# A four-layer trunk on one core: group 0 of each squared-ReLU layer as plain products, and the attention's output projection in three parts

## The chip, the cores and the metric

The kernel runs on one core of one Trainium2 chip. The metric is the device time of one execution in microseconds (us), lower is better. TensorE (PE) does the matmuls and writes them to the accumulators (PSUM); VectorE (DVE) and ScalarE (ACT) read those and do everything elementwise; SyncE (SP) issues most DMAs. Each engine works through its own queue in order.

## The reference, cut to what matters

Input x has 512 frames of 1024 features. Four residual layers follow each other: attention, squared-ReLU MLP, a recurrent block, squared-ReLU MLP, and at the end a norm. Each sub-layer sees rmsnorm(h), and its output is added to h.

```
def sq_relu_mlp(h, w1, w2):
    z = jax.nn.relu(jnp.einsum('bsd,df->bsf', h, w1))    # 1024 -> 4096
    return jnp.einsum('bsf,fd->bsd', z * z, w2)          # 4096 -> 1024

# attention: 16 heads of 64; o holds all heads, w_o is 1024 x 1024
    return jnp.einsum('bsd,de->bse', o, w_o)

for layer in range(2):
    hn = rmsnorm(h, norm_mix[layer])
    h = h + mix(hn)            # attention in layer 0, the recurrent block in layer 1
    h = h + sq_relu_mlp(rmsnorm(h, norm_mlp[layer]), mlp_w1[layer], mlp_w2[layer])
```

All is float32.

## The kernel before, in words

The residual h lies transposed in eight tiles hT[k] of 128 features x 512 frames (KT = 8, T = 512, U = 256, P = 128). To keep float32 accuracy in the faster matmul type, every operand is split into a high half H (rounded, made by ScalarE) and a low half L (the rest, made by VectorE), and every product is three matmuls: H by H, H by L, L by H. This is mm3, lines 176 to 178, which is why nearly all matmuls carry these lines. The names say which product it is: p for the MLP's up products, d for its down products, wo and ro for the two output projections, qk and v for the attention's projections, s, x and oa for the attention's scores, transposes and sums.

**Weights.** A list, plan, holds all weight units of the program in the order of use. fetch takes the next one: a DMA on SP's queue, the high half wh by ScalarE (line 118), the low half wl by VectorE (line 119). A plain unit is 1024 numbers a partition: four k of 256 columns. The units wait in five slots of the pool wsp; in an MLP there are slots of a second pool, wx, too, and of every nine units the last four go there. want(n) takes n units for a matmul group and first prefetches until state["ahead"] more are ready. state["stop"] is the place in the plan at which the prefetch halts until the next stage sets it anew.

**The MLP.** mlp runs over eight groups g of 512 hidden features. up(g) makes the group's hidden features z; down(g-1, m) for eight m adds the group before to hT[m]. They alternate, so that TensorE has down products while VectorE and ScalarE finish z. up uses a Strassen-like scheme (Winograd's form): features and frames are cut in two, and seven products of 256 columns (names "1" to "7") take the place of eight. For this some units of weights are sums of blocks, which VectorE adds beforehand (kinds s1 to s4, lines 115 and 116, tiles b, in the single-buffered pool sr), and the moving operands of some products are sums of blocks of the normed input (sums_of, tiles tH and tL). One of the four sums, t1, is made in the norm's split instead: with blocks=True, lines 204 to 207 write the difference of the two halves of frames into the second half of hnH and hnL for the first four k. The products are put together by seven adds on VectorE, rectified and scaled by rstd r (relu2, line 577), squared, and split.

**The norm.** Norm.feed(k) splits hT[k] times the gain as soon as it is complete. The squares (square, line 220) are added into one tile (nm1acc in layer 0, nm2acc in layer 1); sums adds them over the features with eight tiny matmuls (nm1ss), and rstd turns the result into a row (nm1row). The up products do without rstd until they are rectified. In layer 0's and layer 1's MLP sums and rstd are called inside up(0), and mlp begins with prefetch(4), the four sums_of and then the eight squares.

**The attention.** For head i the loop calls score(i), turn(i-1) (softmax's transposes) and weigh(i-2) (the products with v). After each of the three it calls fill(FILL), which hands a credit to a queue of other matmul work: the projections for later heads and the output projection. A step of a qk or wo projection (three matmuls of 512 columns) costs 2 credits, one of v (three of 256) costs 1. An item of the queue starts only when a head has been reached (its gate); need(name) forces an item to its end.

```
queue += wo_("woA", (0, 1, 2, 3), U, False) + wo_("woB", (4, 5, 6, 7), U, True)
```

woA multiplies the first four head pairs by their rows of w_o and adds the result to hT; its gate is weigh(7). woB does the last four pairs, its gate is weigh(15), the last head; after each of its outputs it feeds the MLP's norm.

The order of the instructions on each engine is laid out at compile time by a program, which starts from the order of these calls and moves an instruction when what it needs isn't there yet. The order quoted in times below is the one that ran.

Of the kernel before, what the change touches and what calls it, by code (L numbers as in the profile page):

```python
# [10 lines left out]
F32 = mybir.dt.float32  # L11
# [4 lines left out]
P = 128  # L16
# [8 lines left out]

FILL = 7.6

# [13 lines left out]
def trunk(ctx: ExitStack, tc: tile.TileContext, xT, cols, win, wqkv, wo, rwin, rga, rgx, rwo, w1, w2, out):  # L41
# [44 lines left out]
    def fetch():  # L86
# [4 lines left out]
        if state["more"] is not None:  # L91
            pool = state["more"] if state["units"] % 9 >= 5 else wsp
            state["units"] += 1
# [58 lines left out]
    def add_mlp(layer):  # L152
        starts.append(len(plan))
        for g in range(9):
            if g < 8:
                rows, cs = (slice(0, T), slice(T, D)), (slice(g * T, g * T + U), slice(g * T + U, (g + 1) * T))
                srcs = [w1[layer][rows[k], cs[c]] for k, c in ((0, 0), (0, 1), (1, 1), (1, 0))]
                up_ = [(kind, 4, srcs) for kind in ("11", "s1", "12", "22", "s2", "s4", "s3")]
            else:
                up_ = []  # L160
            dn = [("plain", 4, [w2[layer][(g - 1) * T : g * T, u * U : (u + 1) * U]]) for u in range(4)] if g else []
            if up_ and dn:
                plan.extend(up_[0:2] + dn[0:1] + up_[2:3] + dn[1:2] + up_[3:5] + dn[2:3] + up_[5:7] + dn[3:4])
            else:
                plan.extend(up_ + dn)

# [5 lines left out]
    add_mlp(1)  # L172
    state["stop"] = starts[0]

# [16 lines left out]
    class Norm:  # L191
        def __init__(self, name, gain, c0=0, n=T, blocks=False):
            self.name, self.gain, self.acc, self.last, self.c, self.n = name, gain, None, None, slice(c0, c0 + n), n
            self.blocks, self.psum = blocks, mmp if blocks else atp

        def split(self, k):
            g = cst[:, self.gain + k : self.gain + k + 1]
            if not self.blocks or k >= KT // 2:
                S.activation(hnH[k], hT[k], AF.Copy, scale=g)
                V.scalar_tensor_tensor(hnL[k], hT[k], g, f(hnH[k]), ALU.mult, ALU.subtract)  # L200
                return

            d = wk.tile([P, T], F32, name=f"{self.name}d{k}", tag="nsq", bufs=2)[:, :U]
            V.tensor_sub(d, hT[k][:, LO], hT[k][:, HI])
            for src, c in ((hT[k][:, LO], LO), (d, HI)):
                S.activation(hnH[k][:, c], src, AF.Copy, scale=g)
                V.scalar_tensor_tensor(hnL[k][:, c], src, g, f(hnH[k][:, c]), ALU.mult, ALU.subtract)

# [13 lines left out]
        def feed(self, k):  # L222
            if k == 0:
                tc.keep_in_program_order(S.activation(spare, epsb, AF.Sqrt))
            self.split(k)
            if not self.blocks:
                self.square(k)


        def sums(self):  # L230
            nt = self.n // P
            ss = self.psum(f"{self.name}ss")
            parts = [self.acc] if self.last is None else [self.acc, self.last]
            for t in range(nt):
                for n, part in enumerate(parts):
                    PE.matmul(
                        ss[:, 2 * t : 2 * t + 2], part[:, t * P : (t + 1) * P], ones[:, 0:2],
                        start=n == 0, stop=n == len(parts) - 1,
                    )
            S.activation(rt[:, :nt], ss[:, 0 : 2 * nt : 2], AF.Sqrt, bias=epsb, scale=1.0 / D)  # L240
            V.reciprocal(rt[:, :nt], rt[:, :nt])

        def rstd(self):
            nt = self.n // P
            row = self.psum(f"{self.name}row")
# [10 lines left out]
    nm1 = Norm("nm1", C_MLP0, blocks=True)  # L256
    with ExitStack() as actx:
# [214 lines left out]
        for i in range(NH + 2):  # L472
# [17 lines left out]
            fill(FILL)  # L490
        need("woB")

# [37 lines left out]
    def mlp(ly, norm, nxt, halves):  # L530
        with ExitStack() as mctx:
            pool = lambda name, bufs: mctx.enter_context(tc.tile_pool(name=f"{name}{ly}", bufs=bufs))
            sr, wx, tp, cp, zp = pool("sr", 1), pool("wx", 4), pool("t", 1), pool("c", 1), pool("z", 2)
            state.update(raw=sr, more=wx, units=0, ahead=7, stop=starts[ly + 1] if ly + 1 < len(starts) else None)
            prefetch(4)
            z, r, tH, tL = {}, [], [], []

            def sums_of(k):
                g, g2 = (cst[:, norm.gain + j : norm.gain + j + 1] for j in (k, k + 4))
                a = wk.tile([P, T], F32, name=f"ha{ly}{k}", tag="nsq", bufs=2)  # L540
                S.activation(a, hT[k], AF.Copy, scale=g)
                H = tp.tile([P, 3, U], F32R, name=f"tH{ly}{k}", tag=f"tH{k}")
                L = tp.tile([P, 3, U], F32R, name=f"tL{ly}{k}", tag=f"tL{k}")
                raw = cp.tile([P, 2, T], F32, name=f"ht{ly}{k}", tag="cB" if k % 2 else "cA")
                raw = raw.rearrange("p i (j c) -> p (i j) c", j=2)

                V.scalar_tensor_tensor(raw[:, 2], hT[k + 4][:, HI], g2, a[:, HI], ALU.mult, ALU.subtract)
                V.tensor_add(raw[:, 1], raw[:, 2], a[:, LO])
                V.scalar_tensor_tensor(raw[:, 0], hT[k + 4][:, LO], g2, raw[:, 1], ALU.mult, ALU.subtract)
                S.activation(H[:, 0:2], raw[:, 0:2], AF.Copy, scale=-1.0)  # L550
                V.scalar_tensor_tensor(L[:, 0:2], raw[:, 0:2], -1.0, f(H[:, 0:2]), ALU.mult, ALU.subtract)  # L551
                S.copy(H[:, 2], raw[:, 2])
                V.tensor_sub(L[:, 2], raw[:, 2], f(H[:, 2]))
# [10 lines left out]
            B11, t1, B21, B22 = own(0, LO), own(0, HI), own(4, LO), own(4, HI)  # L564
            t4, t2, t3 = (sum_(n) for n in range(3))

# [8 lines left out]

            def relu2(g, n, c, op, rr_):
                V.scalar_tensor_tensor(c, c, 0.0, rr_[:, None, :].to_broadcast([P, 2, T]), op, ALU.mult)
                S.activation(c, c, AF.Square)
# [4 lines left out]
                for i in range(2):  # L583
                    z[g, 2 * n + i] = (zH[:, i], zL[:, i])

            def up(g):

                acc = {}

                def one(n, xs):  # L590
                    acc[n] = (mmp if g == 0 and n in "54" else atp)(f"p{n}{ly}{g}")
                    product(acc[n], xs)
                    acc[n] = pair(acc[n])
# [19 lines left out]
                V.tensor_add(cA[:, :, HI], acc["3"], cA[:, :, HI])  # L613
                relu2(g, 0, cA, ALU.max, r[0])
                yield
# [3 lines left out]
                V.tensor_add(cB[:, :, HI], acc["5"], w)  # L619
                relu2(g, 1, cB, ALU.min, r[0])  # L620
                yield
# [59 lines left out]

    nm2 = Norm("nm2", C_MLP1, blocks=True)
    with ExitStack() as rctx:
# [172 lines left out]
```

## Time and profile before

| what | value |
|---|---|
| median of 3 runs | 1104.23 us (1103.11 to 1105.21) |
| the profiled execution's own time | 1108.84 us |
| its span | 1107.1 us |
| mean granted TensorE clock | 0.989 |
| weight units fetched as plain in the MLPs | 64 (512 KB each) |
| weight blocks fetched to be summed in the MLPs | 64 (512 KB each) |

The profile comes from one execution, so sums are made against 1108.84 us. In a view of stretches each row has the window, its length, then for each engine the busy time and the number of instructions, the TensorE clock that was granted (PEclk, 1.00 is full speed), the share of the DMA engines and GB/s. With a tile's name as filter only instructions that touch this tile are counted. Matmuls are pipelined: one lasts longer than the step to the next, so the step from start to start is what counts, and a "busy" TensorE can be slow. The group lines have line, engine, operation, output<-input, shapes, count, then busy us and mean ns of one, then the idle time before them with what ended it. The waits have total us, number of times and the longest.

### The profile page before, as it was taken

How to read it: one execution, taken by the hardware profiler on the slowest of the kernel's cores; microseconds unless marked ns; L12 is line 12 of the kernel's file. 1: busy time of each engine (PE TensorE's matmuls, PEld its weight loads, DVE VectorE, ACT ScalarE, POOL GpSimd, SP SyncE). 2: the span in 40 equal slices, each digit the busy share in tenths (PEclk: the TensorE clock that was granted, in tenths of full speed). 3: DMA queues.
4: the chain of work that ended last, by engine and by line, in shares of the span. 5: the costliest groups of instructions: out<-in, count | busy, mean ns of one | idle time of the engine just before them, and what ended most of it. 6: DMA issues, size and time to landing. Idle time of an engine off the chain costs nothing.

```text
span 1107.1 us, 16096 instructions
## 1 busy us (share of the span) xinstructions
PE 1080.5 (98%) x6424; PEld 962.2 (87%) x6424; DVE 875.9 (79%) x1316; ACT 538.5 (49%) x794; POOL 11.0 (1%) x28
## 2 busy tenths in 40 slices
PE   9999999997999999999999999899999999999996
PEld 7889988887899899999988888789899999899996
DVE  7998888788886886777767689988897786777655
ACT  7766665465443443433435497456453343343321
POOL 1000000000000000000000000000000000000000
PEclk9999999998999999999999999999999999999998
DMA  8532441332334324313241122432433333323102
GB/s 266 136 101 72 115 118 55 109 100 77 100 92 152 96 62 138 105 58 115 59 151 58 58 76 77 123 124 82 129 107 103 116 95 94 106 82 99 57 1 77
DMA packets 113786, 109.10 MB, mean 99 GB/s; under 512 B 4016, under 2 KB 110640, under 8 KB 113712
## 3 DMA queue, kind: packets, MB, share of 16 engines
q1 hardware_dynamic: 113568, 108.02, 32.2%
q8 instruction: 50, 0.82, 0.3%
q14 instruction: 24, 0.20, 0.1%
q10 hardware_dynamic: 144, 0.07, 0.0%
HBM read 101.78 MB, written 2.10 MB: 94 GB/s over the span
## 4 chain that ended last, share of the span: by engine, by line
PE 82%; DVE 11%; DMA 3%; ACT 2%; issue 2%; SPq 0%; DVEq 0%; ACTq 0%
PE d L176 10%; PE d L177 10%; PE d L178 10%; PE p L176 9%; PE p L178 9%; PE p L177 9%; DVE wl L119 2%; PE x L384 1%; PE xb L176 1%; PE xb L178 1%; PE xb L177 1%; ACT wh L118 1%; DMA wr<-in_wqkv 1%; PE v L176 1%; PE oa L400 1%
## 5 line engine op out<-in xcount | busy, mean ns | idle before, releaser
L118 ACT CAST wh<-b 128x1024 fp32r<-128x1024 f32 x112 | 115.9, 1049 | 203.1 <-DVE b L116 76.8
L177 PE MATMUL d<-zL,wh 128*128 128x512 f32 (+1 forms) x544 | 205.9, 379 | 0.0
L176 PE MATMUL d<-zH,wh 128*128 128x512 f32 (+1 forms) x544 | 205.3, 380 | 0.0
L178 PE MATMUL d<-zH,wl 128*128 128x512 f32 (+1 forms) x544 | 204.7, 377 | 0.0
L119 DVE TENSOR_TENSOR wl<-b,wh 128x1024 fp32r<-128x1024 f32 x112 | 135.6, 1223 | 48.0 <-ACT wh L118 48.0
L118 ACT CAST wh<-wr 128x1024 fp32r<-128x1024 f32 (+1 forms) x121 | 125.7, 1041 | 94.7 <-PE p L177 45.6
L119 DVE TENSOR_TENSOR wl<-wr,wh 128x1024 fp32r<-128x1024 f32 (+1 forms) x121 | 146.8, 1213 | 21.7 <-ACT wh L118 21.5
L176 PE MATMUL p<-hnH,wh 128*128 128x256 f32 x512 | 147.2, 288 | 4.8 <-ACT wh L118 3.9
L178 PE MATMUL p<-hnH,wl 128*128 128x256 f32 x512 | 147.0, 287 | 2.1 <-DVE wl L119 2.1
L177 PE MATMUL p<-hnL,wh 128*128 128x256 f32 x512 | 147.3, 288 | 0.0
L178 PEld LDWEIGHTS d<-zH,wl 128*128 128x128 f32 x544 | 102.4, 188 | 19.2
L176 PEld LDWEIGHTS d<-zH,wh 128*128 128x128 f32 x544 | 102.5, 189 | 16.8 <-ACT zH L581 0.4
L631 DVE TENSOR_TENSOR hT<-d,hT 128x512 f32<-128x512 f32 x120 | 82.3, 688 | 43.9 <-PE d L178 43.7
L177 PEld LDWEIGHTS d<-zL,wh 128*128 128x128 f32 x544 | 102.7, 189 | 15.8
L178 PE MATMUL p<-tH,wl 128*128 128x256 f32 x384 | 108.9, 284 | 1.9 <-DVE wl L119 1.9
L176 PE MATMUL p<-tH,wh 128*128 128x256 f32 x384 | 109.2, 284 | 0.6 <-ACT tH L550 0.6
L177 PE MATMUL p<-tL,wh 128*128 128x256 f32 x384 | 108.8, 284 | 0.5 <-DVE tL L551 0.5
L176 PEld LDWEIGHTS p<-hnH,wh 128*128 128x128 f32 x512 | 100.3, 196 | 7.2 <-ACT wh L118 4.3
L178 PEld LDWEIGHTS p<-hnH,wl 128*128 128x128 f32 x512 | 100.2, 196 | 2.5 <-DVE wl L119 2.5
L177 PEld LDWEIGHTS p<-hnL,wh 128*128 128x128 f32 x512 | 100.4, 196 | 1.7
L176 PEld LDWEIGHTS p<-tH,wh 128*128 128x128 f32 x384 | 73.9, 193 | 2.5 <-ACT tH L550 0.8
L177 PEld LDWEIGHTS p<-tL,wh 128*128 128x128 f32 x384 | 73.7, 192 | 2.5 <-DVE tL L551 0.7
(331 smaller groups left out, 2065.8 us busy)
## 6 DMA issues: line engine op xcount, KB each, us to landing
wr<-in_w SPq DMA_DIRECT2D x64, 512.0 KB, 3.5
b<-in_w SPq DMA_DIRECT2D x64, 512.0 KB, 4.2
wr<-in_wqkv SPq DMA_DIRECT2D x20, 512.0 KB, 3.9
wr<-in_rwin SPq DMA_DIRECT2D x16, 512.0 KB, 3.5
wr<-in_wo SPq DMA_DIRECT2D x8, 512.0 KB, 3.5
wr<-in_rwo SPq DMA_DIRECT2D x8, 512.0 KB, 3.5
hT<-in_xT SPq DMA_DIRECT2D x8, 256.0 KB, 5.1
bias<-in_win SPq DMA_DIRECT2D x4, 512.0 KB, 4.5
```

Source lines behind the costliest of these rows:

```text
L118: S.copy(H[:, :n], raw[:, :n])
L119: V.tensor_sub(L[:, :n], raw[:, :n], f(H[:, :n]))
L176: PE.matmul(acc, WH, XH, start=start, stop=False)
L177: PE.matmul(acc, WH, XL, start=False, stop=False)
L178: PE.matmul(acc, WL, XH, start=False, stop=stop)
L384: PE.transpose(b[:, c : c + P], pt[:, seg[t] + kt * P : seg[t] + (kt + 1) * P], ident)
L400: PE.matmul(oa[:, T - n :], vv, pH[:, c : c + n], start=False, stop=kt == 3)
L631: V.tensor_add(hT[m], acc, hT[m])
```

## The change

Three things are done together.

**Group 0 of each MLP is computed plainly**: four outputs of 128 features, each over eight k, with matmuls of 512 columns. Its weights become four plain units in place of seven, and the stop of the prefetch before a layer moves four units on, so that these four may be fetched in the stage before. mlp no longer begins with a prefetch; it calls the squares first and then sums_of. sums is called after the first two outputs, rstd after the third. The norm's split has one form for all k; t1 becomes a fourth sum in sums_of, whose raw sums now lie in the slots of the z tiles. The slots of wx go from four to three a tag, units modulo 8 in place of 9, and ahead from 7 to 6 units.

**The output projection gets three parts**: woA as before, woB with pairs 4 and 5 (gate weigh(11)), woC with pairs 6 and 7 (gate weigh(15)), which feeds the norm. The units of woB and woC are two k of 512 columns.

**FILL** goes from 7.6 to 8.28.

```
-FILL = 7.6
+FILL = 8.28
...
-            pool = state["more"] if state["units"] % 9 >= 5 else wsp
+            pool = state["more"] if state["units"] % 8 >= 5 else wsp
...
+    def add_wo(r):
+        for u in range(2):
+            plan.append(("plain", 2, [wo[r * P : (r + 2) * P, u * T : (u + 1) * T]]))
...
-    for r in (0, T):
-        for u in range(4):
-            add(wo, r, u * U, 4)
+    for u in range(4):
+        add(wo, 0, u * U, 4)
+    add_wo(4), add_wo(6)
...
         for g in range(9):
+            if g == 0:
+                add(w1[layer], 0, 0, KT)
+                add(w1[layer], 0, U, KT)
+                continue
...
-    state["stop"] = starts[0]
+    state["stop"] = starts[0] + 4
...
         def split(self, k):
             g = cst[:, self.gain + k : self.gain + k + 1]
-            if not self.blocks or k >= KT // 2:
-                S.activation(hnH[k], hT[k], AF.Copy, scale=g)
-                V.scalar_tensor_tensor(hnL[k], hT[k], g, f(hnH[k]), ALU.mult, ALU.subtract)
-                return
-
-            d = wk.tile([P, T], F32, name=f"{self.name}d{k}", tag="nsq", bufs=2)[:, :U]
-            V.tensor_sub(d, hT[k][:, LO], hT[k][:, HI])
-            for src, c in ((hT[k][:, LO], LO), (d, HI)):
-                S.activation(hnH[k][:, c], src, AF.Copy, scale=g)
-                V.scalar_tensor_tensor(hnL[k][:, c], src, g, f(hnH[k][:, c]), ALU.mult, ALU.subtract)
+            S.activation(hnH[k], hT[k], AF.Copy, scale=g)
+            V.scalar_tensor_tensor(hnL[k], hT[k], g, f(hnH[k]), ALU.mult, ALU.subtract)
...
-        queue += wo_("woA", (0, 1, 2, 3), U, False) + wo_("woB", (4, 5, 6, 7), U, True)
+        queue += wo_("woA", (0, 1, 2, 3), U, False) + wo_("woB", (4, 5), T, False) + wo_("woC", (6, 7), T, True)
...
-            sr, wx, tp, cp, zp = pool("sr", 1), pool("wx", 4), pool("t", 1), pool("c", 1), pool("z", 2)
-            state.update(raw=sr, more=wx, units=0, ahead=7, stop=starts[ly + 1] if ly + 1 < len(starts) else None)
-            prefetch(4)
+            sr, wx, tp, cp, zp = pool("sr", 1), pool("wx", 3), pool("t", 1), pool("c", 1), pool("z", 2)
+            state.update(raw=sr, more=wx, units=0, ahead=6, stop=starts[ly + 1] + 4 if ly + 1 < len(starts) else None)
...
+                V.tensor_sub(raw[:, 3], a[:, LO], a[:, HI])
                 V.scalar_tensor_tensor(raw[:, 2], hT[k + 4][:, HI], g2, a[:, HI], ALU.mult, ALU.subtract)
                 V.tensor_add(raw[:, 1], raw[:, 2], a[:, LO])
                 V.scalar_tensor_tensor(raw[:, 0], hT[k + 4][:, LO], g2, raw[:, 1], ALU.mult, ALU.subtract)
+                S.copy(H[:, 2:4], raw[:, 2:4])
+                V.tensor_sub(L[:, 2:4], raw[:, 2:4], f(H[:, 2:4]))
...
-            for k in range(4):
-                sums_of(k)
-            for k in range(KT):
-                norm.square(k)
...
-            for n, _ in enumerate(up(0)):
-                if n == 1:
-                    norm.sums()
-                if n == 2:
-                    r.append(norm.rstd())
+            xs = [(hnH[k], hnL[k]) for k in range(KT)]
+            for k in range(KT):
+                norm.square(k)
+            for k in range(4):
+                sums_of(k)
+            cs = [cp.tile([P, 2, T], F32, name=f"c{n}{ly}0", tag=f"c{n}") for n in "AB"]
+            for n in range(2):
+                WH, WL = want(2)
+                accs = [mmp(f"u{ly}{2 * n + i}") for i in range(2)]
+                if n == 0:
+                    project(accs, PAIR, WH, WL, xs)
+                    norm.sums()
+                    first = accs
+                    continue
+                for i in range(2):
+                    project(accs[i : i + 1], PAIR[i : i + 1], WH, WL, xs)
+                    if i == 0:
+                        r.append(norm.rstd())
+                        for j in range(2):
+                            V.scalar_tensor_tensor(cs[0][:, j], first[j], 0.0, r[0], ALU.max, ALU.mult)
+                        square(0, 0, cs[0])
+                    V.scalar_tensor_tensor(cs[1][:, i], accs[i], 0.0, r[0], ALU.max, ALU.mult)
+                square(0, 1, cs[1])
```

The eight tiny matmuls of sums and of rstd move from the PSUM tag of the projections ("mm") to the other one ("at").

More of the change, by code (lines that the diff above doesn't have):

```diff
@@ L160, in add_mlp @@
                 up_ = []
-            dn = [("plain", 4, [w2[layer][(g - 1) * T : g * T, u * U : (u + 1) * U]]) for u in range(4)] if g else []
-            if up_ and dn:
+            dn = [("plain", 4, [w2[layer][(g - 1) * T : g * T, u * U : (u + 1) * U]]) for u in range(4)]
+            if up_:
                 plan.extend(up_[0:2] + dn[0:1] + up_[2:3] + dn[1:2] + up_[3:5] + dn[2:3] + up_[5:7] + dn[3:4])
             else:
-                plan.extend(up_ + dn)
+                plan.extend(dn)
     add_mlp(0)
@@ L225, in feed @@
             self.split(k)
-            if not self.blocks:
+            if not self.late:
                 self.square(k)
@@ L231, in sums @@
             nt = self.n // P
[L232 removed]
+            ss = atp(f"{self.name}ss")
             parts = [self.acc] if self.last is None else [self.acc, self.last]
@@ L244, in rstd @@
             nt = self.n // P
-            row = self.psum(f"{self.name}row")
+            row = atp(f"{self.name}row")
             for t in range(nt):
@@ L255, in trunk @@
     n0 = Norm("n0", C_MIX0)
-    nm1 = Norm("nm1", C_MLP0, blocks=True)
+    nm1 = Norm("nm1", C_MLP0, late=True)
     with ExitStack() as actx:
@@ L490, in trunk @@
             fill(FILL)
-        need("woB")
+        need("woC")
     ap = cst[:, C_AP : C_AP + KT]
@@ L541, in sums_of @@
                 S.activation(a, hT[k], AF.Copy, scale=g)
-                H = tp.tile([P, 3, U], F32R, name=f"tH{ly}{k}", tag=f"tH{k}")
-                L = tp.tile([P, 3, U], F32R, name=f"tL{ly}{k}", tag=f"tL{k}")
-                raw = cp.tile([P, 2, T], F32, name=f"ht{ly}{k}", tag="cB" if k % 2 else "cA")
+                H = tp.tile([P, 4, U], F32R, name=f"tH{ly}{k}", tag=f"tH{k}")
+                L = tp.tile([P, 4, U], F32R, name=f"tL{ly}{k}", tag=f"tL{k}")
+                raw = zp.tile([P, 2, T], F32, name=f"ht{ly}{k}", tag=("zH0", "zH1", "zL0", "zL1")[k])
                 raw = raw.rearrange("p i (j c) -> p (i j) c", j=2)
+                V.tensor_sub(raw[:, 3], a[:, LO], a[:, HI])
                 V.scalar_tensor_tensor(raw[:, 2], hT[k + 4][:, HI], g2, a[:, HI], ALU.mult, ALU.subtract)
@@ L549, in sums_of @@
                 V.scalar_tensor_tensor(raw[:, 0], hT[k + 4][:, LO], g2, raw[:, 1], ALU.mult, ALU.subtract)
+                S.copy(H[:, 2:4], raw[:, 2:4])
+                V.tensor_sub(L[:, 2:4], raw[:, 2:4], f(H[:, 2:4]))
                 S.activation(H[:, 0:2], raw[:, 0:2], AF.Copy, scale=-1.0)
                 V.scalar_tensor_tensor(L[:, 0:2], raw[:, 0:2], -1.0, f(H[:, 0:2]), ALU.mult, ALU.subtract)
-                S.copy(H[:, 2], raw[:, 2])
-                V.tensor_sub(L[:, 2], raw[:, 2], f(H[:, 2]))
                 tH.append(H)
                 tL.append(L)
-            for k in range(4):
-                sums_of(k)
-            for k in range(KT):
-                norm.square(k)
             own = lambda k0, c: [(hnH[k0 + k][:, c], hnL[k0 + k][:, c]) for k in range(4)]
             sum_ = lambda n: [(tH[k][:, n], tL[k][:, n]) for k in range(4)]
-            B11, t1, B21, B22 = own(0, LO), own(0, HI), own(4, LO), own(4, HI)
-            t4, t2, t3 = (sum_(n) for n in range(3))
+            B11, B21, B22 = own(0, LO), own(4, LO), own(4, HI)
             def product(acc, xs):
@@ L584, in relu2 @@
                     z[g, 2 * n + i] = (zH[:, i], zL[:, i])
+            def relu2(g, n, c, op):
+                V.scalar_tensor_tensor(c, c, 0.0, r[0][:, None, :].to_broadcast([P, 2, T]), op, ALU.mult)
+                square(g, n, c)
             def up(g):
@@ L590, in one @@
                 def one(n, xs):
-                    acc[n] = (mmp if g == 0 and n in "54" else atp)(f"p{n}{ly}{g}")
+                    acc[n] = atp(f"p{n}{ly}{g}")
                     product(acc[n], xs)
@@ L613, in up @@
                 V.tensor_add(cA[:, :, HI], acc["3"], cA[:, :, HI])
-                relu2(g, 0, cA, ALU.max, r[0])
+                relu2(g, 0, cA, ALU.max)
                 yield
@@ L619, in up @@
                 V.tensor_add(cB[:, :, HI], acc["5"], w)
-                relu2(g, 1, cB, ALU.min, r[0])
+                relu2(g, 1, cB, ALU.min)
                 yield
@@ L633, in down @@
                     nxt(m)
-            for n, _ in enumerate(up(0)):
-                if n == 1:
-                    norm.sums()
-                if n == 2:
-                    r.append(norm.rstd())
+            xs = [(hnH[k], hnL[k]) for k in range(KT)]
[9 more added lines that the diff above has]
+                    project(accs, PAIR, WH, WL, xs)
+                    norm.sums()
+                    first = accs
[9 more added lines that the diff above has]
+                square(0, 1, cs[1])
+            t4, t2, t3, t1 = (sum_(n) for n in range(4))
             for g in range(1, 8):
@@ L679, in trunk @@
     mlp(0, nm1, n1.feed, False)
-    nm2 = Norm("nm2", C_MLP1, blocks=True)
+    nm2 = Norm("nm2", C_MLP1, late=True)
     with ExitStack() as rctx:
```

7 lines of the change are left out of this document (3 added, 4 removed).

## The prediction, on record before the run

> **What bounds the kernel now.** I read the page's busy shares first.
>
> ```profile
> PE 1080.5 (98%) x6424; PEld 962.2 (87%) x6424; DVE 875.9 (79%) x1316; ACT 538.5 (49%) x794; POOL 11.0 (1%) x28
> ```
>
> TensorE looks full, so the kernel seems bound by its count of matmuls, and this change adds matmul time. But these are means over stages. The stretches view, cut at the start of each MLP layer, against a stretch in the middle of layer 0, says more.
>
> ```profile
> core 0 of [0], span 1107.1 us
> core 0: us, PE busy (x) PEld busy (x) DVE busy (x) ACT busy (x) POOL busy (x), PEclk, DMA share, GB/s
> 249.70:299.80 50.10, 42.64 (x279) 40.45 (x278) 43.26 (x61) 28.67 (x39) 0.00 (x0) 0.86 0.28 85
> 751.60:792.70 41.10, 38.70 (x289) 37.36 (x287) 37.46 (x46) 23.80 (x30) 0.00 (x0) 0.96 0.33 103
> 231.50:271.20 39.70, 33.99 (x190) 29.41 (x189) 38.95 (x64) 25.57 (x41) 0.00 (x0) 0.95 0.26 81
> 270.00:275.00 5.00, 5.00 (x25) 5.00 (x25) 1.42 (x5) 0.48 (x2) 0.00 (x0) 0.50 0.68 226
> 300.00:400.00 100.00, 100.00 (x628) 90.65 (x627) 79.06 (x85) 36.98 (x37) 0.00 (x0) 1.00 0.37 112
> ```
>
> In the middle of a layer (last row) TensorE never stops, at full clock, and VectorE is 79% busy. In the first 50.1 us of layer 0's MLP TensorE is idle for 7.5 us and has a mean clock of 0.86, in layer 1's first 41.1 us idle for 2.4 us at 0.96. Just ahead, from 231.5 to 271.2, VectorE is busy for 38.95 of 39.7 us: there it sets the pace. The waits of TensorE by what ended them confirm it:
>
> ```profile
> PE p L178 <- DVE wl L119: 4.0, 3, 1.9
> PE p L176 <- ACT wh L118: 3.9, 2, 2.2
> ...
> PE s L353 <- DMA kl<-kl: 1.4, 1, 1.4
> ```
>
> The group's products (p) wait for the halves of a weight: wl is made by VectorE, and wh by ScalarE from sums that VectorE makes first. To see what these starts lose I need matmuls per stretch (first the products p, then the down products d, then the eight tiny sums of a norm) and their steps at full pace.
>
> ```profile
> 249.70:299.80 50.10, 35.23 (x241) 0.86 0.28 85
> 751.60:792.70 41.10, 32.94 (x251) 0.96 0.33 103
> ```
>
> ```profile
> 249.70:299.80 50.10, 5.59 (x21) 0.86 0.28 85
> 751.60:792.70 41.10, 5.16 (x21) 0.96 0.33 103
> ```
>
> ```profile
> 751.60:792.70 41.10, 1.05 (x8) 0.96 0.33 103
> ```
>
> ```profile
> 249.71 0.28 PE L176 MATMUL p<-hnH,wh 128*128 128x256 f32 x1
> ...
> 258.33 0.28 PE L176 MATMUL p<-tH,wh 128*128 128x256 f32 x1
> ```
>
> ```profile
> 563.94 0.40 PE L176 MATMUL d<-zH,wh 128*128 128x512 f32 x1
> ...
> 566.69 0.28 PE L176 MATMUL p<-hnH,wh 128*128 128x256 f32 x1
> ```
>
> Between the first pair lie 72 products: 8.62/72 = 0.120 us per step of 256 columns. Between the second lie 12 down products: 2.75/12 = 0.229 us per step of 512. At that pace the first stretch needs 241 x 0.120 + 21 x 0.229 + 2 x 1.05 (sums and the row of rstd) = 35.8 us and takes 50.1, so layer 0 loses **14.3 us**. Layer 1 needs 251 x 0.120 + 4.8 + 2.1 = 37.0 of 41.1 and loses **4.1 us**. This, 18.4 us, is what the change can win there.
>
> **Term 1, TensorE's own work.** Group 0's seven products in two halves, four k and three matmuls are 168 of 256 columns: 168 x 0.120 = 20.2 us. As plain products they are four outputs, eight k, three matmuls: 96 of 512 columns, 96 x 0.229 = 22.0 us. All of it lies on the path: **+1.8 us a layer, +3.6**. The plain form with hn as moving operand isn't in this stage; the nearest row is d, of the same width. Upper bound: twice the 256-column step, 96 x 0.240 = 23.0, +2.8 a layer.
>
> The Trainium skill (TensorE: Matmul & The Clock Gate, section Wait — 56ns, not 53.3ns?) gives a warm step of N/2.4 ns and about 2.5 ns more. An estimate from it is 109 ns for 256 columns and 216 ns for 512, which makes the added work 96 x 0.216 - 168 x 0.109 = 2.4 us a layer, and the sum below -10.8. The steps here are 120 and 229 ns, and the trace decides.
>
> **Term 2, VectorE's work at the start of layer 0.** Its groups between 231.5 and 271.2 us:
>
> ```profile
> L119 DVE TENSOR_TENSOR wl<-b,wh 128x1024 fp32r<-128x1024 f32 x7 | 8.6, 1227 | 0.7 <-ACT wh L118 0.7
> L335 DVE TENSOR_TENSOR hT<-wo,hT 128x512 f32<-128x512 f32 x8 | 5.5, 686 | 0.9 <-PE wo L178 0.9
> L220 DVE TENSOR_TENSOR nm1acc<-nm1acc,nm1sq 128x512 f32<-128x512 f32 x7 | 4.9, 702 | 0.0
> L116 DVE TENSOR_TENSOR b<-b,b 128x1024 f32<-128x1024 f32 x3 | 3.7, 1228 | 0.0
> L200 DVE SCALAR_TENSOR_TENSOR hnL<-hT,cst,hnH 128x512 fp32r<-128x512 f32 x4 | 3.0, 749 | 0.0
> L551 DVE SCALAR_TENSOR_TENSOR tL<-ht,tH 128x512 fp32r<-128x512 f32 x4 | 2.8, 697 | 0.0
> L549 DVE SCALAR_TENSOR_TENSOR ht<-hT,cst,ht 128x256 f32<-128x256 f32 x4 | 2.0, 489 | 0.0
> L547 DVE SCALAR_TENSOR_TENSOR ht<-hT,cst,ha 128x256 f32<-128x256 f32 x4 | 1.9, 488 | 0.0
> L207 DVE SCALAR_TENSOR_TENSOR hnL<-nm1d,cst,hnH 128x256 fp32r<-128x256 f32 x4 | 1.9, 478 | 0.0
> L207 DVE SCALAR_TENSOR_TENSOR hnL<-hT,cst,hnH 128x256 fp32r<-128x256 f32 x4 | 1.9, 478 | 0.0
> L553 DVE TENSOR_TENSOR tL<-ht,tH 128x256 fp32r<-128x256 f32 x4 | 1.7, 430 | 0.0
> L548 DVE TENSOR_TENSOR ht<-ht,ha 128x256 f32<-128x256 f32 x4 | 1.7, 428 | 0.0
> L204 DVE TENSOR_TENSOR nm1d<-hT 128x256 f32<-128x256 f32 x4 | 1.7, 419 | 0.0
> ```
>
> ```profile
> 269.93 0.70 DVE L220 TENSOR_TENSOR nm1acc<-nm1acc,nm1sq 128x512 f32<-128x512 f32 x1
> 270.53 0.70 DVE L604 TENSOR_TENSOR cA<-p,w 128x512 f32<-128x512 f32 x1
> ```
>
> Queued operations overlap: the second row starts 0.60 us after the first, not 0.70. I take 0.1 us off each duration. Per layer the change takes from group 0 three weight splits and four weight sums, 7 x 1.13 = 7.9 us, and the seven adds that put the products together, 7 x 0.60 = 4.2. The first four norm splits lose (0.32 + 2 x 0.38 - 0.65) x 4 = 1.7. It adds a fourth sum t1 in the kernel's sums_of, which costs a subtraction (0.32) and a 512-wide low half in place of a 256-wide one (0.59 - 0.33): 0.6 x 4 = 2.3. The rectifying goes from two 1024-wide to four 512-wide operations, 2.4 against 2.3. Sum: **-11.4 us of VectorE a layer**. Besides, group 0's four units are plain, so up to four splits (4.5 us) and their DMAs may go ahead of the layer: the stop of the prefetch moves four units on.
>
> What is late next? Count from the start T of the last output projection, woC: 48 matmuls, 11.0 us by the step of 0.229. Then the first plain unit takes 11.0 us (to T+22), the sums 1, the second 11.0 and rstd 1 (to T+35), then group 1's products at 2.9 us each. VectorE has after T: eight residual adds and low halves, 8 x (0.59 + 0.65) = 9.9 us; say two late splits of group 0, 2.3; seven squares' adds, 4.2; four sums_of, 4 x (0.32 + 0.39 + 0.33 + 0.39 + 0.59 + 0.60) = 10.5; group 1's first two units with two weight sums, 4 x 1.13 = 4.5; the four rectifications and two zL, 4.7. That is 36.1 us by T+38, when TensorE asks for the second product's operands, and the squares are done by about T+17, 5 us before their sums. So VectorE keeps up, with 2 us to spare, and I stay nearer the lower end: I leave **2.5 us** of waits in layer 0 (bounds 0.5, ordinary handovers, and 6, a debt in which the four sums_of run ahead of the rectifying) and **0.7 us** in layer 1 (0.2 to 2.5), where the recurrent block's last outputs are 5.5 us apart (24 x 0.229) and VectorE starts without a queue. Gains: 14.3 - 2.5 = **11.8** and 4.1 - 0.7 = **3.4**.
>
> **The clock.** At 270 to 275 us TensorE ran at 0.50 though busy, right after its waits; in the 50.1 us the clock alone took 0.14 x 50.1 = 7.0 us, nearly half of the loss. If the waits go, so does this. The Trainium skill (TensorE: Matmul & The Clock Gate, on HAM oscillation) states as its rule no idle gaps of TensorE over about 3.4 us. By that rule no wait that I leave lowers the clock, and the first rival below would be 3.5 us better, 1094.7. The trace disagrees: no wait of p exceeded 2.2 us, yet the clock halved. So several short waits close together suffice, and the rivals count the clock with the waits.
>
> **Term 3, the attention's end.** The output projection's count of matmuls is unchanged (96 + 48 + 48). The second half of it is split by pairs, so eight residual adds are new: 8 x 0.59 = 4.7 us of VectorE, beside matmuls, in a stage where it has gaps (two in the rows below), nothing. If that cover were gone, at most 4.7. The parts of two pairs are fetched as two 512-wide pieces each, the same eight DMAs of 512 KB on SP's queue. The pair 4 and 5 part (woB) may fill TensorE's waits from head 11 on. FILL is the credit that each of three fills a head hands to the queue of projections. Up to pair 6's keys stand 256 credits (v0 to v2 and five pairs at 32 each): 256/7.6 = 33.7 fills, in head 11's turn, just ahead of head 12 that needs them; 256/8.28 = 30.9, in head 10's. The wait of s for kl above is for such keys: **-1.4 us** (0 to 1.4). Against it: woC starts with pairs 6 and 7, and after the last head's products pair 7 must still be formed.
>
> ```profile
> 228.54 0.69 DVE L406 TENSOR_TENSOR o<-oa,ax 64x512 f32<-64x512 f32 x1 [0.79 <-ACT ax L405]
> 229.92 0.69 DVE L411 TENSOR_TENSOR oL<-o,oH 128x512 fp32r<-128x512 f32 x1 [0.69 <-ACT oH L410]
> ```
>
> From 228.54 to 230.61 that is 2.1 us. Before, the first output's pairs 4 to 6 covered it (9 x 0.229 = 2.1); now pair 6 of one output covers 0.7, unless other outputs' pair 6 go first. **+1.0 us** (0 to 2.1).
>
> **The smaller edits** (weight slots 9 to 8, six units ahead for seven, units modulo 8, norm tiles in the other PSUM tag) cost nothing while the middle of a layer has VectorE idle for 21 of 100 us and TensorE never idle: what hides them is that lead.
>
> **Sum** against the profiled execution, 1108.84 us (span 1107.1): +3.6 - 11.8 - 3.4 - 1.4 + 1.0 = **-12.0**, so 1096.8. It stands 4.6 above the median of the three runs, 1104.23; the same -12.0 from there gives **1092.2 us**. Best ends: +3.6 - 13.8 - 3.9 - 1.4 = -15.5, 1088.7. Worst ends: +5.6 - 8.3 - 1.6 + 2.1 = -2.2, 1102.0, which needs all at once.
>
> **Rivals.**
> *Half the stall moves on.* Sums_of and group 1's weights come due together, and waits move from group 0 to group 1. For: my margin is a few us in 36. Against: 11.4 us less work. Priced at half of the old losses left, 7.2 + 2.0 in place of 2.5 + 0.7, it gives -6.0, 1098.2 us, and with woC's wait at its upper end 1099.3. Chance 0.17.
> *The norm's sum is asked for too early: slower.* The sums now stand 11 us behind the group's first matmul, in TensorE's order ahead of the second unit; before, the last add to nm1acc ended at 270.63, 20.9 us behind the first product (249.71). If it stays that late, layer 0's TensorE waits 9.9 us there, and the clock loss of 7.0 us comes back with it: +16.9 in place of the 2.5 left, -12.0 + 14.4 = +2.4, 1106.6 us. It turns the sign when the last add ends over 18.5 us behind the first matmul (7.5 of wait and 7.0 of clock). For: the queue was full for 40 us. Against: the squares now stand ahead of sums_of in the program, and need 4.2 us. Chance 0.08.
> *The smaller lead starves the groups: slower.* One slot fewer, and each of 14 later groups waits 1.3 us: +18.2, 1110.4. It decides once the lead in the middle of a layer is under one unit, (7 x 2.9 + 8 x 2.75)/11 = 3.8 us; the 100 us without a wait speak against it. Chance 0.04.
> *The edit doesn't do what it says*, because the order of work is laid out by a program and the plain units aren't split ahead: that ends in the first rival.
>
> **Numbers.** The forecast has 0.68, the rest 0.03 is better than its best end. About 0.2%, 2.2 us, is what a measurement of this kernel can tell from no change. Faster: 0.68 + 0.03 + 0.15 = 0.86; same 0.04 (ends of two rivals); slower 0.10. The forecast's own range is 1088 to 1098; with the first rival, 1088 to 1101, which leaves out the slower rivals and the corners.
>
> **What would show it.** In the changed profile, at the start of both MLPs: PEclk at 1.0, TensorE's idle time under 3 us in layer 0, no 40 us stretch of full VectorE, products of 512 columns where 168 of 256 were, the norm's sums about 11 us behind the first of them without a wait, the wait of s for kl gone, and at most one wait of some 1 us for oL. I am wrong if the sums wait, if group 1's products wait for wl or tL, if PEclk falls below 0.9 over either start, or if waits show in the middle of a layer.

## The result: 5.3 us faster, less than half of what was forecast

| kernel | median us | range | ratio to before, 95% interval |
|---|---|---|---|
| before, beside the changed one | 1104.72 | 1103.11 to 1105.52 | |
| changed | 1099.38 | 1099.18 to 1099.47 | 0.9953 (0.9936 to 0.997) |

The forecast was -12.0 us from the median, 1092.2, with a range of 1088 to 1098. The profiled execution of the changed kernel took 1099.47 us (span 1097.7), so it stands at its median, where the one of before stood 4.6 above it. Both are answered below.

The page first. TensorE has 144 matmuls fewer (two layers of 168 - 96), and VectorE works 13.9 us less.

```profile
PE 1076.9 (98%) x6280; PEld 952.2 (87%) x6280; DVE 862.0 (79%) x1292; ACT 533.3 (49%) x778; POOL 10.4 (1%) x28
```

The stretches of the forecast, in the changed kernel (window, length, then busy us and instructions of PE, PEld, DVE, ACT and POOL, clock, DMA):

```profile
core 0 of [0], span 1097.7 us
249.70:299.80 50.10, 44.54 (x242) 38.93 (x241) 46.04 (x65) 27.39 (x38) 0.00 (x0) 0.93 0.30 92
751.60:792.70 41.10, 41.10 (x243) 36.46 (x242) 35.98 (x49) 22.55 (x27) 0.00 (x0) 1.00 0.35 108
241.50:277.00 35.50, 30.04 (x135) 24.29 (x133) 35.50 (x58) 25.64 (x38) 0.00 (x0) 0.96 0.29 88
274.30:281.20 6.90, 4.10 (x19) 4.10 (x20) 6.90 (x10) 1.22 (x2) 0.00 (x0) 0.51 0.22 76
300.00:400.00 100.00, 100.00 (x630) 90.78 (x629) 74.95 (x81) 38.85 (x39) 0.00 (x0) 1.00 0.31 96
```

Layer 1's start is clean: 41.10 of 41.10 us busy at full clock, where before lost 4.1 us. The middle of a layer is as full as before. But layer 0's start still has TensorE idle for 5.6 us, and a clock of about a half from 274.3 to 281.2. VectorE is busy for the whole 35.5 us from 241.5 to 277. The waits of TensorE name a new one, in a single piece, and those of the products p for wl and wh and of s for kl are gone from the list:

```profile
PE nm1row L247 <- DVE rt L241: 5.6, 1, 5.6
PE ro L184 <- ACT gdH L778: 1.6, 1, 1.6
```

The row of rstd (nm1row) waits for a reciprocal of 128 x 4 numbers. The order of time on ScalarE, VectorE and TensorE shows why:

```profile
265.29 0.27 ACT L240 ACTIVATE rt<-nm1ss,epsb 128x4 f32<-128x4 f32 x1 [0.61 <-PE nm1ss L236]
```

```profile
263.24 0.69 DVE L220 TENSOR_TENSOR nm1acc<-nm1acc,nm1sq 128x512 f32<-128x512 f32 x1
263.84 0.42 DVE L546 TENSOR_TENSOR ht<-ha 128x256 f32<-128x256 f32 x1
...
276.27 0.69 DVE L553 SCALAR_TENSOR_TENSOR tL<-ht,tH 128x512 fp32r<-128x512 f32 x1
276.87 0.18 DVE L241 RECIPROCAL rt<-rt 128x4 f32<-128x4 f32 x1
```

```profile
264.31 0.95 PE L236 MATMUL nm1ss<-ones,nm1acc 128*128 128x2 f32 x8
...
271.15 0.39 PE L186 MATMUL u<-hnH,wl 128*128 128x512 f32 x1
277.10 1.22 PE L247 MATMUL nm1row<-ident,rt 128*128 128x128 f32 x4 [5.56 <-DVE rt L241]
```

The square root is there at 265.56. The reciprocal takes 0.18 us, but it stands in VectorE's queue behind the sums_of (ht, tL), and runs 11.3 us later. TensorE ends its last plain product (u) at 271.54, and the row stands next in its queue, ahead of group 1's products. The wait costs 5.6 us; of the 6.9 us at half clock that begin during it TensorE is busy for 4.10, which costs some 2.0 us more. Together that is 7.6 us.

### The profile page after: what moved, and what is told of

Read it like the earlier page. It is cut to its first block, busy times and chain, and to the rows that moved or that the text cites. A ratio compares the mean times of both kernels' runs of the same rounds, so it can differ in the third digit from the quotient of the medians.

```text
span 1097.7 us, 15793 instructions
## 1 busy us (share of the span) xinstructions
PE 1076.9 (98%) x6280; PEld 952.2 (87%) x6280; DVE 862.0 (79%) x1292; ACT 533.3 (49%) x778; POOL 10.4 (1%) x28
## 4 chain that ended last, share of the span: by engine, by line
PE 88%; DVE 7%; DMA 2%; ACT 2%; issue 1%; SPq 0%; DVEq 0%; ACTq 0%
PE d L184 11%; PE d L185 10%; PE d L186 10%; PE p L186 9%; PE p L185 9%; PE p L184 9%; PE x L384 2%; PE xb L184 1%; PE xb L186 1%; PE wo L184 1%; PE xb L185 1%; DMA wr<-in_wqkv 1%; PE wo L185 1%; PE wo L186 1%; PE ro L185 1%
## 5 line engine op out<-in xcount | busy, mean ns | idle before, releaser
L119 DVE TENSOR_TENSOR wl<-b,wh 128x1024 fp32r<-128x1024 f32 x98 | 118.8, 1222 | 34.0 <-ACT wh L118 33.9
L186 PE MATMUL p<-tH,wl 128*128 128x256 f32 x448 | 126.8, 283 | 0.0
L185 PE MATMUL p<-tL,wh 128*128 128x256 f32 x448 | 126.8, 283 | 0.0
L184 PE MATMUL p<-tH,wh 128*128 128x256 f32 x448 | 126.6, 282 | 0.0
L184 PE MATMUL p<-hnH,wh 128*128 128x256 f32 x336 | 95.5, 284 | 0.0
L185 PE MATMUL p<-hnL,wh 128*128 128x256 f32 x336 | 95.5, 284 | 0.0
L186 PE MATMUL p<-hnH,wl 128*128 128x256 f32 x336 | 95.5, 284 | 0.0
L186 PEld LDWEIGHTS p<-tH,wl 128*128 128x128 f32 x448 | 85.8, 192 | 0.0
L184 PEld LDWEIGHTS p<-hnH,wh 128*128 128x128 f32 x336 | 64.9, 193 | 1.6
L185 PEld LDWEIGHTS p<-hnL,wh 128*128 128x128 f32 x336 | 64.9, 193 | 1.6
```

The lines of the kernel that those rows point to most:

```text
L119: V.tensor_sub(L[:, :n], raw[:, :n], f(H[:, :n]))
L184: PE.matmul(acc, WH, XH, start=start, stop=False)
L185: PE.matmul(acc, WH, XL, start=False, stop=False)
L186: PE.matmul(acc, WL, XH, start=False, stop=stop)
```

## The experiments

Ratios are to before, run on the same chip with them.

### The kernel before, once more

> The kernel before, unchanged, profiled once more. Theory A: the profiled execution of before (1108.84 us, mean clock 0.989, 16.9 us at half clock after the start) was some 4 us slower than its usual ones, because short waits at the start of the MLPs sometimes halve TensorE's clock for longer. Then this profile comes out near 1104 us, with the same waits at layer 0's start (TensorE idle about 7.5 us between 250 and 300) and 3 to 10 us less time at half clock. Rival: the first profile was typical and carries about 4.6 us over the timed runs; then this one is near 1108.8 us with the same clock.

Measured 1105.13 us (1102.34 to 1106.33) against 1105.21 (1102.42 to 1107.99) of before beside it, ratio 0.9994 (0.9983 to 1.0006); the profiled execution took 1106.33, clock 0.989 as in the first. Half right. This execution is 2.5 us faster than the first profile though it, too, has 17.1 us at half clock after the start: here in one piece (from 261.0), there in pieces of 10.24, 3.41 and 3.41 us, the last two right behind single waits of 1.74 and 2.18 us. So for these two profiles neither theory holds as it was put: what differs is where the half clock falls, not how much of it there is. From one timed execution to the next the amount differs too, as theory A has it: those of before with a mean clock of 0.994 or more took 1102.3 to 1103.7 us, those at 0.989 took 1104.6 to 1108.0. The kernel's timed runs spread over 5.7 us. The first profile, at 1108.84, lay above all of them, and a forecast that takes a loss out of such an execution takes out too much.

### The attention's part alone, and the MLP's part alone

The first is before with this:

```
-FILL = 7.6
+FILL = 8.28
-        queue += wo_("woA", (0, 1, 2, 3), U, False) + wo_("woB", (4, 5, 6, 7), U, True)
+        queue += wo_("woA", (0, 1, 2, 3), U, False) + wo_("woB", (4, 5), T, False) + wo_("woC", (6, 7), T, True)
```

> Before with the second part of the change alone: output projection in three parts and FILL 8.28. Theory A (the gain is all in the MLPs' first groups): within 1.5 us of before, 1103 to 1106 us; the wait of s for kl (1.4 us) is gone, the clock's losses at layer 0's start stay. Rival (the three parts relieve layer 0's start too, since fewer residual adds and norm splits are queued there): 3 us or more faster than before.

The second is the changed kernel with exactly these lines taken back.

> The change without its attention part: group 0 plain, smaller pools, but woA and woB with four pairs each and FILL 7.6. Theory A: 1099 to 1101 us, nearly all of the gain, with the wait of nm1row for the reciprocal still there (5 us or less, as woB's outputs come 2.7 us apart and VectorE has more done when they end). Rival (the attention part carries half of the gain): 1102 us or more.

| kernel | median us | range | ratio, 95% interval |
|---|---|---|---|
| attention's part alone | 1113.96 | 1113.42 to 1114.82 | 1.0083 (1.0066 to 1.0099) |
| MLP's part alone | 1092.68 | 1092.22 to 1093.2 | 0.989 (0.9871 to 0.9908) |

The MLP's part alone gives -12.5 us, the whole of the forecast and more than the whole change. The attention's part costs 8.8 us alone and 6.7 us on top of the MLP's. I had expected neither sign: it was to be worth -0.4, and both runs lie outside the ranges that I had given for them. Alone it makes the old waits at layer 0's start longer (before had 3.7 and 3.9 in the profile taken beside it):

```profile
PE p L182 <- DVE wl L119: 9.0, 3, 5.1
PE p L180 <- ACT wh L118: 5.2, 3, 2.2
```

And the MLP's part without it has no wait there at all, in either layer:

```profile
core 0 of [0], span 1090.9 us
249.70:299.80 50.10, 50.10 (x287) 44.08 (x286) 44.19 (x62) 28.11 (x35) 0.00 (x0) 1.00 0.31 96
751.60:792.70 41.10, 41.10 (x254) 36.98 (x253) 33.14 (x38) 19.14 (x21) 0.00 (x0) 1.00 0.40 129
```

### The same work, the reciprocal earlier in the queue

```
-            for k in range(4):
-                sums_of(k)
...
                     norm.sums()
                     first = accs
+                    for k in range(4):
+                        sums_of(k)
```

> The changed kernel with one move: the four sums_of are called after norm.sums instead of before the first plain unit, so that the norm's reciprocal (4 elements) stands ahead of nearly all of them in VectorE's queue. Nothing is added or left out. Theory A (the missing gain of layer 0 is the 5.6 us wait of nm1row for a reciprocal that stands behind 11 us of other work, and the 6.8 us at half clock after it, 3.4 us): that wait goes, the clock stays at 1.0 over layer 0's start, and the time falls by 5 to 9 us to 1090.5 to 1094.5. Rival (VectorE is simply behind there, whatever the order): the wait moves to the first products of group 1 (tL or wl), and the time stays within 2 us of 1099.4.

Measured 1091.66 us (1091.55 to 1091.94), ratio 0.9881 (0.9865 to 0.9896): 7.7 us faster than the changed kernel, against the 7.6 read from its trace. The reciprocal now runs 0.4 us after the square root began (265.02 here), and nothing waits:

```profile
265.43 0.17 DVE L241 RECIPROCAL rt<-rt 128x4 f32<-128x4 f32 x1
```

```profile
core 0 of [0], span 1090.1 us
249.70:299.80 50.10, 50.10 (x285) 43.97 (x284) 46.32 (x66) 29.58 (x40) 0.00 (x0) 1.00 0.33 100
```

VectorE has the same work (46.32 against 46.04 us in this stretch), so it wasn't simply behind.

### The reciprocal on another engine

The run before moved other work along. Here VectorE's order is left, and the four numbers go to GpSimd:

```
+            if self.late:
+                G.tensor_tensor(rt[:, :nt], rt[:, :nt], minus[:, :nt], ALU.pow)
+            else:
                 V.reciprocal(rt[:, :nt], rt[:, :nt])
```

> The changed kernel, but the reciprocal of the MLP norms (128 x 4 numbers) is done by GpSimd as a power of -1 instead of by VectorE; VectorE's other work keeps its order. Theory A (the wait is the reciprocal's place in VectorE's queue): the row of rstd no longer waits 5.6 us, no half clock at layer 0's start, 1090.5 to 1094 us, like the run with the sums_of called later. Rival (that run was faster because its VectorE order was better elsewhere): 1097 us or more, with the wait moved to VectorE's rectifying or to group 1's products.

Measured 1091.61 us (1091.19 to 1091.85), ratio 0.9887 (0.9873 to 0.99). GpSimd takes 1.36 us for what VectorE does in 0.18, and it is still worth 7.8 us:

```profile
264.99 1.36 POOL L244 TENSOR_TENSOR rt<-rt,minus 128x4 f32<-128x4 f32 x1 [93.73 <-ACT rt L242]
```

```profile
PE nm1row L252 <- POOL rt L244: 0.7, 1, 0.7
```

With this the place of the reciprocal in VectorE's queue is shown to be what the changed kernel pays for at layer 0's start.

### FILL or the three parts

The MLP's part with FILL 8.28 but four pairs in woB; and the changed kernel with FILL 7.6.

> Group 0 plain with woA and woB of four pairs each (as in the run with the MLP part alone, 1092.7 us), and FILL at 8.28. Theory A (the attention part costs through woC: the norm's eight feeds come in the last 11 us instead of 22 us of the projection; FILL itself is harmless): layer 0's start stays without a wait, the wait of s for kl goes, and the time is 1090 to 1093 us. Rival (FILL 8.28 uses up the filling work too early, and that costs the 6.7 us): 1097 us or more, with waits around 200 to 230 us.

> The changed kernel with FILL back at 7.6. Theory A: the wait of nm1row for the reciprocal stays at 4 to 7 us and the time at 1098 to 1101 us. Rival (FILL is the cost): 1092 to 1095 us.

| kernel | median us | range | ratio, 95% interval |
|---|---|---|---|
| MLP's part, FILL 8.28, two parts | 1091.34 | 1091.19 to 1091.62 | 0.9886 (0.987 to 0.9901) |
| MLP's part, FILL 7.6, three parts | 1096.91 | 1096.51 to 1097.88 | 0.9936 (0.9923 to 0.9948) |

FILL is worth -1.3 us with two parts (1092.68 to 1091.34): the wait for kl, 0.9 us there, is gone, and TensorE is idle for 1.1 us less in the first 200 us (196.27 us busy, then 197.40). The three parts cost +8.0 us at FILL 8.28 and +4.2 at 7.6, where the wait of nm1row is 3.7 us; 1096.91 is outside both of my ranges, and why FILL makes the wait longer I haven't tested. Why the third part costs is seen in when the norm is fed. In the two-part kernel the first residual add, the last low half, the last add of the squares and the reciprocal stand so, with the first plain product below them:

```profile
230.62 0.69 DVE L335 TENSOR_TENSOR hT<-wo,hT 128x512 f32<-128x512 f32 x1 [0.86 <-PE wo L186]
...
250.93 0.74 DVE L207 SCALAR_TENSOR_TENSOR hnL<-hT,cst,hnH 128x512 fp32r<-128x512 f32 x1
251.59 0.68 DVE L220 TENSOR_TENSOR nm1acc<-nm1acc,nm1sq 128x512 f32<-128x512 f32 x1
...
265.13 0.17 DVE L241 RECIPROCAL rt<-rt 128x4 f32<-128x4 f32 x1
```

```profile
248.38 0.39 PE L184 MATMUL u<-hnH,wh 128*128 128x512 f32 x1
```

In the changed kernel:

```profile
241.48 1.89 DVE L335 TENSOR_TENSOR hT<-wo,hT 128x512 f32<-128x512 f32 x3 [0.84 <-PE wo L186]
...
250.16 2.74 DVE L207 SCALAR_TENSOR_TENSOR hnL<-hT,cst,hnH 128x512 fp32r<-128x512 f32 x4
```

```profile
248.54 0.47 PE L184 MATMUL u<-hnH,wh 128*128 128x512 f32 x1
```

The norm's work begins 17.8 us before the first plain product in the one and 7.1 us in the other: it starts 10.9 us later, about the 11.0 us of the 48 matmuls that now run ahead of it. From the first plain product TensorE has 22.8 us of work before it must have the row. The reciprocal comes 16.8 us after that product in the one, 28.3 in the other. Meanwhile VectorE is idle for part of the time (230 to 241.5 us: 7.15 of 11.5 us busy).

```profile
230.00:241.50 11.50, 11.12 (x53) 8.93 (x52) 7.15 (x12) 4.32 (x6) 0.00 (x0) 1.00 0.45 141
```

The last add of the squares ends at 252.27 in the one and at 263.93 in the other.

### The middle part behind the last head

```
-("w", 2 * pairs[-1] + 1)
+("w", 15 if name == "woB" else 2 * pairs[-1] + 1)
```

> The changed kernel with the gate of woB moved from head 11 to the last head, so that 22 us of projection stand behind the last head, as before, but the norm's feeds still come in the last 11 us, in woC. Theory A (what counts is how long before the first plain product the feeds begin): the wait of nm1row stays, 4 to 7 us. On top TensorE loses its filling in the last heads, 1 to 4 us: 1100 to 1104 us. Rival (what counts is matmul time behind the last head, whatever it feeds): the wait of nm1row falls under 1 us.

Measured 1096.11 us (1095.49 to 1097.83), ratio 0.993 (0.9918 to 0.9943), faster than theory A said, with a wait that fits neither. It is halved, and neither gone nor the same:

```profile
PE nm1row L247 <- DVE rt L241: 2.8, 1, 2.8
```

```profile
core 0 of [0], span 1094.3 us
249.70:299.80 50.10, 46.39 (x257) 39.93 (x256) 45.23 (x64) 27.61 (x38) 0.00 (x0) 1.00 0.28 85
```

So the late feeds leave a wait by themselves, but part of the price lies in something else that comes earlier when the last head ends earlier. That this is group 1's weights, whose tiles become free with the attention's, is only argued. The expected loss of filling in the last heads did not show: from 200 to 250 us TensorE is busy for 49.96 us.

### The smaller edits alone

```
-            pool = state["more"] if state["units"] % 9 >= 5 else wsp
+            pool = state["more"] if state["units"] % 8 >= 5 else wsp
-            sr, wx, tp, cp, zp = pool("sr", 1), pool("wx", 4), pool("t", 1), pool("c", 1), pool("z", 2)
+            sr, wx, tp, cp, zp = pool("sr", 1), pool("wx", 3), pool("t", 1), pool("c", 1), pool("z", 2)
-            state.update(raw=sr, more=wx, units=0, ahead=7, stop=starts[ly + 1] if ly + 1 < len(starts) else None)
+            state.update(raw=sr, more=wx, units=0, ahead=6, stop=starts[ly + 1] if ly + 1 < len(starts) else None)
```

> Before with the smaller edits alone: three slots a tag in wx for four, units modulo 8 for 9, six units ahead for seven. Theory A (the lead is ample): within 1.5 us of before, no wait between 310 and 580 us and between 810 and 1080 us. Rival (the smaller lead adds to the debt at the start of the layers): 2 us or more slower, with the waits of p for wl and wh at both starts longer.

Measured 1102.55 us (1099.9 to 1103.9), ratio 0.9976 (0.9966 to 0.9987), so 2.6 us faster than before: neither theory. The middles of the layers stay without a wait. At layer 0's start the clock is 0.93, where the two profiles of before have 0.86 and 0.83, and after the start 10.2 us in all are at half clock, where both of before have 17.1:

```profile
core 0 of [0], span 1100.9 us
249.70:299.80 50.10, 44.02 (x309) 41.68 (x308) 45.40 (x62) 29.30 (x39) 0.00 (x0) 0.93 0.32 99
```

A smaller lead asks for fewer weights just when VectorE has a debt. That this is the reason is argued, not shown.

### The best of these and the later sums_of

The two-part kernel with FILL 8.28, and the sums_of called later.

> Group 0 plain, FILL 8.28, woA and woB of four pairs each (1091.3 us), and the sums_of called after norm.sums. Theory A (with four pairs in the last part nothing waits at layer 0's start, so the order no longer matters): 1090.5 to 1092 us, no change. Rival (the reciprocal's place costs something hidden there too): 1089.5 us or less.

Measured 1091.5 us (1091.32 to 1091.66), ratio 0.9883 (0.9867 to 0.99), against 1091.34: no change, as theory A has it. With two parts nothing waits for the reciprocal, although without the move it, too, stands behind the sums_of (265.13, 4.6 us after the end of the square root at 260.52). The version to keep is group 0 plain with FILL 8.28 and two parts: 13.3 us under before and 8.0 under the change.

## Why the prediction was right or wrong, point by point

- **TensorE's own work** (+1.8 us a layer). Right, as far as layer 0 shows it. In the MLP's part alone the 96 plain products and 16 tiny matmuls run from 249.87 to 273.52 us. From the first of each eight tiny ones to the product behind them are 0.8 us. Without these the products take 22.0 us, as forecast, against 20.2 for the seven products. The estimate of +2.4 from the steps in the Trainium skill (TensorE: Matmul & The Clock Gate, section Wait — 56ns, not 53.3ns?) was farther off.
- **The waits at the MLPs' starts** (-11.8 and -3.4). Right in mechanism: in the MLP's part by itself both stretches are busy throughout at full clock, so that even the 2.5 and 0.7 us are gone that I had left. That the sum of the three MLP terms, +3.6 - 11.8 - 3.4 = -11.6, stands so near to the -12.5 measured is in part luck. The losses were read from an execution 4.6 us above the median, which makes them too large, and the run holds the smaller edits, too, which I had at nothing.
- **What is late next.** This step failed. I counted VectorE's work from the start of woC at 36.1 us, due by T+38, and concluded that VectorE keeps up with 2 us to spare. The trace has 35.5 us without a gap from 241.5 to 277.0, with T = 236.63: T+40. That the length agrees is luck: nine operations on weights (wl, b) stand in it where the list had six, and the rectifications and zL, 4.7 us of the list, come only after it. The conclusion was also drawn from the wrong item. I checked the adds of the squares against the sums and the second product's operands against the end, but not the reciprocal, which the program puts behind the sums_of in the queue, and for which rstd waits at T+35. The adds were late as well (T+17 forecast, T+27 measured, T+22 due, since weights had come between). But there TensorE's order gave way: the sums run 15.8 us behind the first plain product instead of 11, with other plain products ahead of them, and don't wait. Of a new place for a step, every instruction counts, and this one takes 0.18 us. None of the signs of being wrong that I had named was there: the wait fell between them.
- **The attention's end** (-0.4). With two parts FILL gives -1.3 against -1.4; with three the same step costs 2.5 us (1096.91 to 1099.38). The wait after the last head (+1.0) was there and small, 0.4 us. But the term left out what woC does to the norm's feeds, and that is +8.0 us at FILL 8.28, most of it the 7.6 of the wait and the half clock after it. I had the number in hand, since I counted T from woC and never asked what T would be with two parts.
- **The rival in which half the stall moves on.** Its number, 1098.2 to 1099.3 us, is the nearest to the 1099.38 measured, and that is luck. The sums_of and the next weights did come due together on VectorE. But the wait fell on the norm's row, in layer 0 alone, and not on group 1's products in both layers, and half of the old losses was an assumed price.
- **The rival of the norm asked too early.** It came nearest in mechanism: TensorE does wait for a part of the norm, but for the reciprocal and not for the adds of the squares, and it costs 7.6 us where the rival had 16.9, so the change still comes out faster. I gave it 0.08, because the adds alone are 4.2 us.
- **The smaller edits** at nothing: -2.6 us by themselves on the old kernel. Whether that remains in the changed one, where the debt is gone, wasn't tried.
- **From the profile to the median.** I took the profiled execution's losses one to one. Profile against profile the change brings 1108.84 - 1099.47 = 9.4 us; median against median 5.3. Of the missing 6.7 us, 4.0 are this difference (9.37 - 5.34). The other 2.7 are two larger errors that partly cancel. Profile against profile the MLP's part gains 16.1 us (1108.84 to 1092.69) where its terms have 11.6, and the attention's part costs 6.8 where its term has -0.4.
- **The clock.** I held that several short waits close together halve it. A single one can. In the profile of before, layer 1's wait of 2.18 us, the only one over 0.3 us there, is followed by 3.41 us at half clock:

```profile
770.00:775.00 5.00, 4.78 (x40) 4.58 (x39) 4.30 (x4) 3.52 (x4) 0.00 (x0) 1.00 0.14 45
775.00:780.00 5.00, 2.82 (x21) 2.62 (x21) 5.00 (x6) 1.76 (x2) 0.00 (x0) 0.94 0.21 73
780.00:785.00 5.00, 5.00 (x33) 5.00 (x33) 5.00 (x6) 3.55 (x5) 0.00 (x0) 0.72 0.35 108
```

So is the wait of 1.74 us at 287.6, with no other in the 17 us before it. In the second profile of before the same two waits, 2.19 and 1.68 us, bring no half clock at all:

```profile
751.60:792.70 41.10, 38.36 (x291) 36.68 (x290) 37.21 (x44) 23.49 (x29) 0.00 (x0) 1.00 0.33 104
```

In the changed kernels one wait of 5.6 us and one of 3.7 brought 6.83 us at half clock each, and one of 2.8 us none (clock 1.00 in the stretch above). So below 3 us the length of a wait doesn't decide by itself; what does, no run here shows. The rule of the Trainium skill (TensorE: Matmul & The Clock Gate, on HAM oscillation), no gaps over about 3.4 us, agrees with these last three waits, but not with the 1.74 and 2.18 us.

## What to carry to other kernels

When a change relieves the engine that sets the pace, follow each tiny instruction that another engine waits for, and ask what stands ahead of it in its queue: 0.18 us of work at the wrong place cost nearly 8 us here. Splitting a part so that less of it is left at the end also takes away the matmuls under which the next stage prepares itself; count that cover from when the feeding begins (17.8 us here, then 7.1). And a loss that is read from one profiled execution is that execution's: take a second profile of a kernel with many waits, or its spread, before subtracting it from a median.

## What the runs showed of the hardware that I had not expected

In all these traces the granted clock after the start is either full or half. The stretches at half last 3.41, 6.83, 10.24 or 17.07 us, multiples of 3.41, besides the last microseconds of every execution. The same short waits bring them in one execution and not in another, and how many there are and where they fall decides a few us: the kernel before spreads over 5.7 us from run to run, the kernels without a wait at the layers' starts over 0.3 to 1.0 us.
